# Forget terms of a forgetting-attention layer: added by VectorE from broadcast rows instead of by TensorE, with the heads' loads in GpSimd's queue

## The chip, the cores and the metric

The kernel runs on one core of one Trainium2 chip. The metric is the device time of one execution in microseconds (us). Engines are named as in the profile: PE is TensorE (PEld its weight loads), DVE is VectorE, ACT is ScalarE, POOL is GpSimd, SP is SyncE. A measurement is the median of several runs.

## The reference

One layer of a hybrid decoder over 512 tokens and 2048 channels, all in float32: a wide input projection feeds a gated short convolution and a forgetting attention with 8 heads of 128 channels; their gated sum is projected back, and a squared-ReLU MLP with 8192 hidden channels follows. The change touches the attention alone:

```
log_f = jax.nn.log_sigmoid(f_logit + b_f)             # (512, 8)
c = jnp.cumsum(log_f, axis=1)                         # per head
...
logits = jnp.einsum('bhqd,bhkd->bhqk', qb, kh) * scale
logits = logits + cb[..., :, None] - c[..., None, :]  # c of the query's row, minus c of the key
logits = jnp.where(causal, logits, -jnp.inf)
p = jax.nn.softmax(logits, axis=-1)
return jnp.einsum('bhqk,bhkd->bhqd', p, vh)
```

## The kernel before, in words

Nearly all the time goes to large matrix products. A product is worked in `Group`s: a group multiplies by a 2048 x 512 piece of weights in the seven-product (Strassen) manner. Its blocks are called A11, A12, A22 and S1 to S4, and each block's product has 48 matmuls of 256 columns (L164, L166 and L168 in `mm_rows` and `mm_cols`, accumulators a to d). A block of weights is loaded on SP's queue (L221), in places summed with another by DVE (L124), and then split into a high part `th` by ACT (L110) and a low part `tl` by DVE (L113, 2.3 us for 2048 columns). DVE adds products from PSUM to results (L127), ACT copies others (L252).

The attention stage lies between 255 and 480 us of the span. Before it, q and k of all heads were stored to DRAM as `kq_d` and v as `v_d`. It begins with the forget logits `fl`: ACT and DVE form their log-sigmoid `lf` (L784 to L787), PE sums it along the sequence by a product with a triangle `ut` (`pc`, L794), and DVE keeps the negative as `ncT` [8 heads, 512] (L796). Its transpose `cn` has the query's own term. `cparts` holds `ncT` in three bfloat16 parts, and `sel` for each head a matrix of ones that picks the head's rows out of it (L810 to L827), so that PE can add the key's term to the scores.

`attend(h)` computes one head. Three loads bring kT, qT and vv, 256 KB each (L837 to L840). For each of four tiles of 128 queries PE forms the scores in a PSUM bank (L846), adds the forget term `sel` x `cparts` (L847) and the causal mask (L848); tile 1 has 128 keys, tile 4 has 512. DVE takes the maximum (L850), ACT the exponential straight from PSUM with the row's sum (L856), DVE the reciprocal and the scaling (L858, L859), PE the transposes (L862, `tp`), DVE copies them to SBUF (`pt`, L864), and PE multiplies by vv into one bank `o` (L866). ACT copies `o` to `ov`, which POOL's queue stores to `a_d` (L869). The score tiles take turns in two banks (5 and 7). All SBUF tiles of `attend` come out of one ring of six buffers (tag "at", L777).

The loop at L948 goes over the conv branch's six groups. Ahead of each of the first four it issues the attention of two heads, so a round of the stage is two heads beside one group. A group stores its results through POOL's queue as `z_d` (L951). The order of instructions on each engine is set by the scheduler, by its own estimates, not by the order in which they are written; each engine and each DMA queue then works in order. The results of the stage are first wanted in later groups.

Of the kernel before, what the change touches and what calls it, by code (L numbers as in the profile page):

```python
# [8 lines left out]
F32 = mybir.dt.float32  # L9
F32R = mybir.dt.float32r  # L10
BF16 = mybir.dt.bfloat16
AF = mybir.ActivationFunctionType
ALU = mybir.AluOpType
AX = mybir.AxisListType

P = 128
S = 512
D = 2048
KT = D // P
NT = S // P  # L20
# [4 lines left out]
NH = AW // P  # L25
DFF = 4 * D
EPS = 1e-6
NEG = -1.0e30
# [17 lines left out]
def tile_hybrid_block(ctx: ExitStack, tc, x, g_mix, w_in, b_f, b_gate, conv_w, w_conv_out,  # L46
                      w_attn_out, w_mix_out, g_mlp, w_ff1, w_ff2, g_final, out):
    nc = tc.nc
    x, out = x[0], out[0]
# [4 lines left out]
    stat = ctx.enter_context(tc.tile_pool(name="stat", bufs=2))  # L54
# [3 lines left out]
    dram = ctx.enter_context(tc.tile_pool(name="dram", bufs=1, space=bass.MemoryType.DRAM))  # L58

    def phase(name):  # L60
        return tc.tile_pool(name=name, bufs=1, reuse_waits="tile")

    def bank(i, name):
        return psum.tile([P, S], F32, tag=f"p{i}", name=name)
# [7 lines left out]


    v_d = dram.tile([NT, P, AW], F32, name="v_d")
    kq_d = dram.tile([2, NH, P, S], F32, name="kq_d")
    z_d = dram.tile([3, CT, P, S], F32, name="z_d")
    g_d = dram.tile([2, KT, P, S], F32, name="g_d")
# [9 lines left out]
    warm = const.tile([P, 1], F32, name="warm")  # L87
# [8 lines left out]
    fl = const.tile([P, NT, NH], F32, name="fl")  # L96
# [605 lines left out]
    a, b = (gV0.acc(k)[0] for k in "ab")  # L702
# [71 lines left out]
    ph = ExitStack()  # L774
    pb = ph.enter_context(phase("pb"))

    def at(name, shape=None, dt=F32):  # L777
        return pb.tile(shape or [P, S], dt, tag="at", name=name, bufs=6)


    fa = const.tile([P, NT, NH], F32, name="fa")
# [1 line left out]
    nc.scalar.activation(out=fa, in_=fa, func=AF.Exp, scale=-1.0)  # L783
    nc.scalar.activation(out=fa, in_=fa, func=AF.Ln, bias=1.0)  # L784
    lf = const.tile([P, NT, NH], F32, name="lf")
    nc.vector.tensor_scalar(out=lf, in0=fl, scalar1=0.0, scalar2=None, op0=ALU.min)
    nc.vector.tensor_tensor(out=lf, in0=lf, in1=fa, op=ALU.subtract)  # L787
    ut = at("ut")
    nc.gpsimd.memset(ut, 1.0)
    nc.gpsimd.affine_select(out=ut[:, :P], in_=ut[:, :P], compare_op=ALU.is_ge, fill=0.0, base=0,  # L790
                            pattern=[[1, P]], channel_multiplier=-1)
    pc = bank(4, "pc")
    for t in range(NT):
        nc.tensor.matmul(pc[:NH, t * P:], lf[:, t, :], ut[:, :S - t * P], start=(t == 0), stop=(t == NT - 1))  # L794
    ncT = at("ncT", [NH, S])
    nc.vector.tensor_scalar(out=ncT, in0=pc[:NH, :], scalar1=-1.0, scalar2=None, op0=ALU.mult)  # L796
    pcn = bank(5, "pcn")
    for t in range(NT):
        nc.tensor.transpose(pcn[:, t * NH:(t + 1) * NH], ncT[:, t * P:(t + 1) * P], ident[:NH, :NH])
    cn = const.tile([P, NT, NH], F32, name="cn")  # L800
    nc.vector.tensor_scalar(out=cn.rearrange("p t h -> p (t h)"), in0=pcn[:, :NT * NH], scalar1=-1.0, scalar2=None,
                            op0=ALU.mult)
    identb = const.tile([P, P], BF16, name="identb")
# [3 lines left out]
    nc.gpsimd.affine_select(out=maskb, in_=maskb, compare_op=ALU.is_ge, fill=NEG, base=0,  # L807
                            pattern=[[-1, P]], channel_multiplier=1)

    cparts = pb.tile([96, S], BF16, name="cparts")  # L810
    nc.gpsimd.memset(cparts, 0.0)
    c1 = at("c1", [NH, S])
    nc.vector.tensor_copy(cparts[0:NH, :], ncT)
    nc.vector.tensor_tensor(out=c1, in0=ncT, in1=cparts[0:NH, :], op=ALU.subtract)
    nc.vector.tensor_copy(cparts[32:32 + NH, :], c1)
    c1b = at("c1b", [NH, S], BF16)
    nc.vector.tensor_copy(c1b, c1)
    c2 = at("c2", [NH, S])
    nc.vector.tensor_tensor(out=c2, in0=c1, in1=c1b, op=ALU.subtract)
    nc.vector.tensor_copy(cparts[64:64 + NH, :], c2)  # L820
    sel = pb.tile([96, NH, P], BF16, name="sel")
    nc.gpsimd.memset(sel, 0.0)

    nc.vector.memset(warm, 1.0)
    for b in range(3):
        nc.scalar.activation(out=sel[32 * b:32 * b + NH, :, :], in_=identb[0:NH, 0:NH].unsqueeze(2).to_broadcast([NH, NH, P]),
                             func=AF.Copy, scale=warm[0:NH, :])  # L827

    mt = [0]

    def m1(name):
# [1 line left out]
        return bank(4 + mt[0] % 4, name)  # L833

    def attend(h):
        kT, qT = at("kT"), at("qT")
        nc.sync.dma_start(out=kT, in_=kq_d[0, h])  # L837
        nc.sync.dma_start(out=qT, in_=kq_d[1, h])
        vv = at("vv", [P, NT, P])
        nc.sync.dma_start(out=vv, in_=v_d[:, :, h * P:(h + 1) * P].rearrange("t p c -> p t c"))  # L840
        o = bank(4, "o")
        for qi in range(NT):
            n = (qi + 1) * P
            qs = slice(qi * P, n)
            sc = bank(5 + 2 * (qi % 2), "sc")
            nc.tensor.matmul(sc[:, :n], qT[:, qs], kT[:, :n], start=True, stop=False)  # L846
            nc.tensor.matmul(sc[:, :n], sel[:, h, :], cparts[:, :n], start=False, stop=False)  # L847
            nc.tensor.matmul(sc[:, qs], identb, maskb, start=False, stop=True)  # L848
            nm = stat.tile([P, 1], F32, tag="nm", name="nm")
            nc.vector.tensor_reduce(out=nm, in_=sc[:, :n], axis=AX.X, op=ALU.max, negate=True)  # L850
            bias = stat.tile([P, 1], F32, tag="bias", name="bias")
            nc.vector.scalar_tensor_tensor(out=bias, in0=nm, scalar=cn[:, qi, h:h + 1], in1=cn[:, qi, h:h + 1],
                                           op0=ALU.subtract, op1=ALU.add)
            p = at("p")
            sm = stat.tile([P, 1], F32, tag="sm", name="sm")
            nc.scalar.activation(out=p[:, :n], in_=sc[:, :n], func=AF.Exp, bias=bias, accum_out=sm)  # L856
            rs = stat.tile([P, 1], F32, tag="rs", name="rs")
            nc.vector.reciprocal(out=rs, in_=sm)  # L858
            nc.vector.tensor_scalar(out=p[:, :n], in0=p[:, :n], scalar1=rs, scalar2=None, op0=ALU.mult)  # L859
            tp = bank(6, "tp")  # L860
            for ki in range(qi + 1):
                nc.tensor.transpose(tp[:, ki * P:(ki + 1) * P], p[:, ki * P:(ki + 1) * P], ident)  # L862
            pt = at("pt")
            nc.vector.tensor_copy(pt[:, :n], tp[:, :n])  # L864
            for ki in range(qi + 1):
                nc.tensor.matmul(o[:, qs], vv[:, ki, :], pt[:, ki * P:(ki + 1) * P], start=(ki == 0), stop=(ki == qi))  # L866
        ov = at("ov")
        nc.scalar.activation(out=ov, in_=o, func=AF.Copy)
        nc.gpsimd.dma_start(out=a_d[h], in_=ov)  # L869

# [76 lines left out]
    n = 0  # L947
    for g in (4, 2, 0, 5, 3, 1):  # L948
        def put_z(i, j, v, g=g, n=n):
            f = 4 * (g % 2) + 2 * j  # L950
            nc.gpsimd.dma_start(out=z_d[g // 2, f:f + 2, :, i * HS:(i + 1) * HS].rearrange("b p c -> p b c"), in_=v)  # L951
            signal(n, i, j, v)

        if n < NH // 2:
            for h in (2 * n, 2 * n + 1):
                attend(h)
        if n == NH // 2:
            ph.close()
            ph = ExitStack()
            pq = ph.enter_context(phase("pq"))  # L960
        ahead(n)
        whole(Group(w_in, g * S, g * S + HS, HS, Q1.moving, mm_cols, steady(n), put_z,
                    extra={} if n < NH // 2 else {"A11": "first", **apart(4, "S2", 0)}))
        behind(n)
        n += 1
# [235 lines left out]
    n = turns[0] + 1  # L1201
# [497 lines left out]
```

## Time and profile before

| | us |
|---|---|
| runs: median of 3 | 2445.77 |
| runs: lowest, highest | 2439.77, 2447.11 |
| the profiled execution's own time | 2440.54 |
| its span in the trace | 2438.7 |
| PE busy in the span | 2407.2 |
| DVE busy | 2043.1 |
| ACT busy | 1205.4 |
| POOL busy | 281.0 |

Rows of the trace read as follows: start in us, duration in us, engine, line, operation, output<-inputs, partitions x elements and type, count. In brackets stands the idle time before and what ended it. A group of instructions has its busy time and the mean in ns of one. The rows of transfers end with the KB of one and the median us from issue to landing. The windows cut the span into stretches and give for each the busy us of every engine, the granted clock of TensorE as a share (PEclk), the share of the DMA engines and GB/s. The chain of waits goes back from the last instruction, at each step to what released it.

### The profile page before, as it was taken

Reading aid. Unit: us, or ns where it says so; the run is one execution under the profiler, and the core shown is the slowest. Engines: PE = TensorE matmul, PEld = TensorE weight load, DVE = VectorE, ACT = ScalarE, POOL = GpSimd, SP = SyncE. Lnnn points to the kernel's source line nnn. Section 1 sums busy time; section 2 is a strip of 40 time slices with the busy share of each in tenths; the row PEclk is TensorE's granted clock in tenths of the full one; section 3 lists DMA queues with packets and bytes.
Section 4 is the critical chain, followed back from the end, with each engine's and each line's share of the span. In section 5 each row is a group of like instructions: output and inputs, shape, how many; then the busy total and the mean of one; then the engine's idle time right before and its main releaser. Section 6 shows DMA issues by size and latency. Waiting matters only on the chain.

```text
span 2438.7 us, 41547 instructions
## 1 busy us (share of the span) xinstructions
PE 2407.2 (99%) x17815; PEld 2263.2 (93%) x17815; DVE 2043.1 (84%) x1715; ACT 1205.4 (49%) x1233; POOL 281.0 (12%) x449
## 2 busy tenths in 40 slices
PE   9999999999999999999999999999999999999998
PEld 9999899999999999899999999999998888888886
DVE  7987777788887778888889888898887888889898
ACT  6444443345455445355656665666655333333334
POOL 1100000111121111113300000000011001100000
PEclk9999999999999999999999999999999999999999
DMA  8565544454656665657854665646587566655662
GB/s 267 176 189 152 155 127 139 139 164 163 212 171 216 210 205 166 218 163 249 318 197 174 219 213 200 233 170 222 210 300 282 166 234 235 231 198 178 245 225 103
DMA packets 283785, 489.89 MB, mean 201 GB/s; under 512 B 11668, under 2 KB 195056, under 8 KB 283216
## 3 DMA queue, kind: packets, MB, share of 16 engines
q1 hardware_dynamic: 232912, 279.01, 36.3%
q0 software_dynamic: 50080, 207.16, 22.8%
q8 instruction: 140, 2.29, 0.4%
q10 hardware_dynamic: 608, 1.06, 0.1%
q14 instruction: 45, 0.37, 0.0%
HBM read 377.60 MB, written 109.05 MB: 200 GB/s over the span
## 4 chain that ended last, share of the span: by engine, by line
PE 87%; DVE 5%; issue 3%; DMA 2%; ACT 1%; POOL 1%; SPq 0%; DVEq 0%; POOLq 0%; ACTq 0%
PE a L168 6%; PE a L164 6%; PE a L166 6%; PE d L168 5%; PE d L164 5%; PE d L166 5%; PE a L187 5%; PE a L185 5%; PE a L183 5%; PE c L164 4%; PE c L166 4%; PE c L168 4%; PE d L187 3%; PE d L185 3%; PE d L183 3%
## 5 line engine op out<-in xcount | busy, mean ns | idle before, releaser
L110 ACT ACTIVATE th<-x 128x2048 fp32r<-128x2048 f32 (+1 forms) x280 | 537.2, 1919 | 514.8 <-DVE x L124 173.9
L113 DVE TENSOR_TENSOR tl<-x,th 128x2048 fp32r<-128x2048 f32 (+2 forms) x282 | 639.5, 2274 | 161.9 <-ACT th L110 146.8
L124 DVE TENSOR_TENSOR x<-x,x 128x2048 f32<-128x2048 f32 (+1 forms) x160 | 366.2, 2288 | 23.7 <-DMA x<-in_w_in_dram 16.7
L110 ACT ACTIVATE th<-y 128x2048 fp32r<-128x2048 f32 (+1 forms) x109 | 185.7, 1704 | 274.3 <-PE a L185 138.6
L113 DVE TENSOR_TENSOR tl<-y,th 128x2048 fp32r<-128x2048 f32 (+1 forms) x109 | 219.1, 2015 | 29.8 <-ACT th L110 29.4
L183 PE MATMUL a<-th,us 128*128 128x512 f32 x512 | 199.3, 389 | 1.3 <-ACT th L110 1.3
L185 PE MATMUL a<-th,us 128*128 128x512 f32 x512 | 199.2, 389 | 0.0
L164 PE MATMUL c<-S,th 128*128 128x256 f32 x848 | 196.6, 277 | 0.7 <-ACT th L110 0.7
L166 PE MATMUL c<-S,th 128*128 128x256 f32 x848 | 196.2, 277 | 0.0
L164 PE MATMUL a<-S,th 128*128 128x256 f32 x784 | 182.2, 278 | 0.8 <-ACT th L110 0.8
L166 PE MATMUL a<-S,th 128*128 128x256 f32 x784 | 180.7, 276 | 0.0
L164 PEld LDWEIGHTS c<-S,th 128*128 128x128 f32 x848 | 159.3, 188 | 1.1 <-ACT th L110 0.8
L166 PEld LDWEIGHTS c<-S,th 128*128 128x128 f32 x848 | 159.3, 188 | 0.0
L164 PEld LDWEIGHTS a<-S,th 128*128 128x128 f32 x784 | 147.2, 188 | 1.0 <-ACT th L110 1.0
L166 PEld LDWEIGHTS a<-S,th 128*128 128x128 f32 x784 | 147.3, 188 | 0.0
L187 PE MATMUL a<-tl,us 128*128 128x512 f32 x512 | 136.9, 389 | 0.6 <-DVE tl L113 0.6
L166 PE MATMUL b<-A,th 128*128 128x256 f32 x544 | 126.6, 278 | 0.0
L164 PE MATMUL b<-A,th 128*128 128x256 f32 x544 | 126.5, 277 | 0.0
L164 PE MATMUL d<-S,th 128*128 128x256 f32 x544 | 126.4, 278 | 0.0
L164 PE MATMUL a<-A,th 128*128 128x256 f32 x544 | 126.2, 277 | 0.0
L166 PE MATMUL a<-A,th 128*128 128x256 f32 x544 | 126.1, 277 | 0.0
L166 PE MATMUL d<-S,th 128*128 128x256 f32 x544 | 125.8, 277 | 0.0
(405 smaller groups left out, 6063.3 us busy)
## 6 DMA issues: line engine op xcount, KB each, us to landing
x<-in_w_in_dram SPq DMA_DIRECT2D x86, 1024.0 KB, 5.8
y<-in_w_ff_dram SPq DMA_DIRECT2D x64, 1024.0 KB, 7.7
x<-in_w_ff_dram SPq DMA_DIRECT2D x60, 1024.0 KB, 8.5
us<-s_d POOLq DMA_DIRECT2D x48, 1024.0 KB, 9.2
s_d<-rh POOLq DMA_DIRECT2D x32, 896.0 KB, 5.7
s_d<-r POOLq DMA_DIRECT2D x32, 896.0 KB, 5.9
x<-in_w_mix_out_dram SPq DMA_DIRECT2D x17, 1024.0 KB, 7.2
g_d<-o POOLq DMA_DIRECT2D x32, 256.0 KB, 2.9
```

The source lines that it names most:

```text
L110: return tied(nc.scalar.activation(out=hi, in_=src, func=AF.Copy))
L113: return tied(nc.vector.tensor_tensor(out=lo, in0=src, in1=hi.bitcast(F32), op=ALU.subtract))
L124: return nc.vector.tensor_tensor(out=out, in0=a, in1=b, op=ALU.subtract)
L164: nc.tensor.matmul(o, hi[:, q, js], Sh, start=first and q == 0 and j == 0, stop=False, skip_group_check=True)
L166: nc.tensor.matmul(o, hi[:, q, js], Sl, start=False, stop=False, skip_group_check=True)
L168: nc.tensor.matmul(o, lo[:, q, js], Sh, start=False, stop=q == nq - 1, skip_group_check=True)
L183: tied(nc.tensor.matmul(o, Sh, hi[:, q, :], start=begin and q == 0, stop=False, skip_group_check=True))
L185: tied(nc.tensor.matmul(o, Sl, hi[:, q, :], start=False, stop=False, skip_group_check=True))
L187: tied(nc.tensor.matmul(o, Sh, lo[:, q, :], start=False, stop=q == nq - 1, skip_group_check=True))
```

## The change

The forget term of a key is no longer added by PE. `ncT` is stored to a DRAM tile `c_d`, and each head loads its row of it laid over all 128 partitions (`cb`). In place of the maximum, DVE runs a `tensor_tensor_reduce`: it computes the negative of (scores + cb), writes it to the SBUF tile `p`, and keeps the row's least in `m`; in the program it is two instructions, the second 128 x 1. The exponential then works within `p` with scale -1. L847, `cparts`, `sel` and their set-up (six DVE and three ACT operations and some memsets) are gone. `lf` is one operation instead of two. kT, qT, cb and vv have one buffer each, `p` and `pt` two each, in place of the ring of six; `ut` and `ncT` use `pt`'s, `ov` uses `p`'s. All loads of a head are in POOL's queue instead of SP's.

```diff
+    c_d = dram.tile([NH, S], F32, name="c_d")
...
-    def at(name, shape=None, dt=F32):
-        return pb.tile(shape or [P, S], dt, tag="at", name=name, bufs=6)
+    def at(tag, name=None, shape=None, bufs=1):
+        return pb.tile(shape or [P, S], F32, tag=tag, name=name or tag, bufs=bufs)
...
-    nc.vector.tensor_scalar(out=lf, in0=fl, scalar1=0.0, scalar2=None, op0=ALU.min)
-    nc.vector.tensor_tensor(out=lf, in0=lf, in1=fa, op=ALU.subtract)
-    ut = at("ut")
+    nc.vector.scalar_tensor_tensor(out=lf, in0=fl, scalar=0.0, in1=fa, op0=ALU.min, op1=ALU.subtract)
+    ut = at("pt", "ut", bufs=2)
...
-    ncT = at("ncT", [NH, S])
+    ncT = at("pt", "ncT", [NH, S], bufs=2)
     nc.vector.tensor_scalar(out=ncT, in0=pc[:NH, :], scalar1=-1.0, scalar2=None, op0=ALU.mult)
+    nc.gpsimd.dma_start(out=c_d, in_=ncT)
...
     def attend(h):
-        kT, qT = at("kT"), at("qT")
-        nc.sync.dma_start(out=kT, in_=kq_d[0, h])
-        nc.sync.dma_start(out=qT, in_=kq_d[1, h])
-        vv = at("vv", [P, NT, P])
-        nc.sync.dma_start(out=vv, in_=v_d[:, :, h * P:(h + 1) * P].rearrange("t p c -> p t c"))
+        kT, qT, cb, vv = at("kT"), at("qT"), at("cb"), at("vv", shape=[P, NT, P])
+        nc.gpsimd.dma_start(out=kT, in_=kq_d[0, h])
+        nc.gpsimd.dma_start(out=qT, in_=kq_d[1, h])
+        nc.gpsimd.dma_start(out=cb, in_=c_d[h:h + 1, :].to_broadcast([P, S]))
+        nc.gpsimd.dma_start(out=vv, in_=v_d[:, :, h * P:(h + 1) * P].rearrange("t p c -> p t c"))
...
-            nc.tensor.matmul(sc[:, :n], sel[:, h, :], cparts[:, :n], start=False, stop=False)
             nc.tensor.matmul(sc[:, qs], identb, maskb, start=False, stop=True)
-            nm = stat.tile([P, 1], F32, tag="nm", name="nm")
-            nc.vector.tensor_reduce(out=nm, in_=sc[:, :n], axis=AX.X, op=ALU.max, negate=True)
+            p = at("p", bufs=2)
+            m = stat.tile([P, 1], F32, tag="nm", name="m")
+            nc.vector.tensor_tensor_reduce(out=p[:, :n], in0=sc[:, :n], in1=cb[:, :n], scale=-1.0, scalar=-NEG, op0=ALU.add,
+                                           op1=ALU.min, accum_out=m)
...
-            p = at("p")
...
-            nc.scalar.activation(out=p[:, :n], in_=sc[:, :n], func=AF.Exp, bias=bias, accum_out=sm)
+            nc.scalar.activation(out=p[:, :n], in_=p[:, :n], func=AF.Exp, bias=bias, scale=-1.0, accum_out=sm)
...
-            pt = at("pt")
+            pt = at("pt", bufs=2)
...
-        ov = at("ov")
+        ov = at("p", "ov", bufs=2)
```

The scheduler also puts the instructions in another order. PE before, in the third round: the second head's first scores (sc_4127, sc_4146) stand among the products of the block S1 (accumulator c), 29 products behind the first head's last output, and each tile has the forget term's product (sel).

```order
L164 MATMUL c_4337<-S1_907,th_4338 128x256
L166 MATMUL c_4337<-S1_907,th_4338 128x256
L846 MATMUL sc_4127<-kT_4120,qT_4121 128x128 [waits DMAHW7_49,DMAHW6_49,Activation_49]
L847 LDWEIGHTS sel_2805
L847 MATMUL sc_4127<-cparts_2794,sel_2805 128x128
L848 LDWEIGHTS identb_2787
L848 MATMUL sc_4127<-maskb_2789,identb_2787 128x128
L846 MATMUL sc_4146<-kT_4120,qT_4121 128x256 [waits Activation_49]
```

PE in the changed program, in the same round: the second head's first scores (sc_4103, sc_4121) stand right behind the first head's second output (o_4006 from pt_4041), among the products of the block A11.

```order
L848 MATMUL o_4006<-pt_4022,vv_4001 128x128 [waits DMASW0_49,DVE_49]
L844 MATMUL tp_4038<-ident_90,p_4028 128x128 x2
L169 MATMUL a_4194<-A11_128,tl_4196 128x256 x6
L848 MATMUL o_4006<-pt_4041,vv_4001 128x128 [waits DVE_49]
L848 MATMUL o_4006<-pt_4041,vv_4001 128x128
L828 MATMUL sc_4103<-kT_4094,qT_4095 128x128 [waits DMASW6_49,DMASW5_49,PE_49]
L829 LDWEIGHTS identb_2788
L829 MATMUL sc_4103<-maskb_2790,identb_2788 128x128
L828 MATMUL sc_4121<-kT_4094,qT_4095 128x256 [waits DVE_49,PE_49]
```

So they moved ahead, past the first head's third and fourth transposes and outputs and most of two blocks of products.

The queues of the loads, SP before: the loads of two heads (kT_4022, kT_4120 and their fellows) stand between the loads of weights (x11 and others).

```order
L837 DMA kT_4022<-kq_d_70 128x512 [waits DMASW4_49,DMASW0_49,PE_49]
L838 DMA qT_4023<-kq_d_70 128x512 [waits DMAHW3_49,DMASW3_49,DMAHW5_49,DMASW2_49,PE_49]
L840 DMA vv_4026<-v_d_69 128x4x128 [waits DMASW3_49,DMAHW4_49,DVE_49,PE_49]
L221 DMA x11_4334<-in_w_in_dram 128x8x256 [waits DVE_49]
L837 DMA kT_4120<-kq_d_70 128x512 [waits DMAHW6_49,DVE_49,PE_49]
L838 DMA qT_4121<-kq_d_70 128x512 [waits DMAHW3_49,DMAHW7_49,DVE_49,PE_49]
L840 DMA vv_4124<-v_d_69 128x4x128 [waits DMAHW0_49,DMAHW2_49,DVE_49,PE_49]
```

POOL in the changed program: the second head's four loads (kT_4094 to vv_4097) follow one another, behind the stores of a group (z_d) and ahead of the first head's store (a_d) and of the next round's loads (kT_4587).

```order
L933 DMA z_d_72<-o_3884 128x2x256 [waits DMASW4_49,DVE_49]
L819 DMA kT_4094<-kq_d_71 128x512 [waits DMASW5_49,PE_49]
L820 DMA qT_4095<-kq_d_71 128x512 [waits DMASW6_49]
L821 DMA cb_4096<-c_d_70 128x512 [waits DMASW7_49,DVE_49]
L822 DMA vv_4097<-v_d_69 128x4x128 [waits DMASW0_49,PE_49]
L851 DMA a_d_78<-ov_4091 128x512 [waits DMASW1_49,Activation_49]
L819 DMA kT_4587<-kq_d_71 128x512 [waits DMASW5_49,DMASW2_49,PE_49]
L820 DMA qT_4588<-kq_d_71 128x512 [waits DMASW6_49,DMASW3_49]
```

So they left SP's queue, which keeps the weights alone, and each of them now waits, by its one buffer, for the engine that last read it for the head before.

More of the change, by code (lines that the diff above doesn't have):

```diff
@@ L808, in tile_hybrid_block @@
                             pattern=[[-1, P]], channel_multiplier=1)
[L810 to L827, printed above, removed]
     mt = [0]
@@ L846, in attend @@
             nc.tensor.matmul(sc[:, :n], qT[:, qs], kT[:, :n], start=True, stop=False)
-            nc.tensor.matmul(sc[:, :n], sel[:, h, :], cparts[:, :n], start=False, stop=False)
             nc.tensor.matmul(sc[:, qs], identb, maskb, start=False, stop=True)
-            nm = stat.tile([P, 1], F32, tag="nm", name="nm")
-            nc.vector.tensor_reduce(out=nm, in_=sc[:, :n], axis=AX.X, op=ALU.max, negate=True)
+            p = at("p", bufs=2)
+            m = stat.tile([P, 1], F32, tag="nm", name="m")
+            nc.vector.tensor_tensor_reduce(out=p[:, :n], in0=sc[:, :n], in1=cb[:, :n], scale=-1.0, scalar=-NEG, op0=ALU.add,
+                                           op1=ALU.min, accum_out=m)
             bias = stat.tile([P, 1], F32, tag="bias", name="bias")
-            nc.vector.scalar_tensor_tensor(out=bias, in0=nm, scalar=cn[:, qi, h:h + 1], in1=cn[:, qi, h:h + 1],
+            nc.vector.scalar_tensor_tensor(out=bias, in0=m, scalar=cn[:, qi, h:h + 1], in1=cn[:, qi, h:h + 1],
                                            op0=ALU.subtract, op1=ALU.add)
-            p = at("p")
             sm = stat.tile([P, 1], F32, tag="sm", name="sm")
-            nc.scalar.activation(out=p[:, :n], in_=sc[:, :n], func=AF.Exp, bias=bias, accum_out=sm)
+            nc.scalar.activation(out=p[:, :n], in_=p[:, :n], func=AF.Exp, bias=bias, scale=-1.0, accum_out=sm)
             rs = stat.tile([P, 1], F32, tag="rs", name="rs")
```

## Prediction

> **What bounds the kernel now.** I read the page's engine shares first, then the waits of TensorE (PE) in the attention stage, which is the only stage that the change touches, and then the stage cut into its four rounds. A round is two heads of attention woven into one group of products for the conv branch; I call the two heads of a round A and B.
>
> ```profile
> PE 2407.2 (99%) x17815; PEld 2263.2 (93%) x17815; DVE 2043.1 (84%) x1715; ACT 1205.4 (49%) x1233; POOL 281.0 (12%) x449
> ```
>
> PE is busy 99% of the 2438.7 us span, so only what PE issues and what it waits for can move the end. In the stage (255 to 480 us) its largest waits are these; the columns are the sum, the count and the longest:
>
> ```profile
> engine line waited for: us in total, times, longest us
> PE sc L846 <- DMA qT<-kq_d: 1.8, 1, 1.8
> PE pc L794 <- DVE lf L787: 1.3, 1, 1.3
> ```
>
> ```profile
> core 0: us, PE busy (x) PEld busy (x) DVE busy (x) ACT busy (x) POOL busy (x), PEclk, DMA share, GB/s
> 264.00:317.00 53.00, 51.23 (x407) 47.11 (x406) 39.79 (x63) 22.32 (x30) 3.31 (x5) 1.00 0.47 145
> 317.00:371.00 54.00, 53.87 (x431) 50.32 (x430) 38.30 (x57) 21.27 (x30) 4.00 (x6) 1.00 0.44 137
> ...
> 425.00:479.00 54.00, 53.72 (x426) 50.00 (x426) 39.03 (x56) 20.72 (x30) 7.41 (x14) 1.00 0.46 141
> ```
>
> So 3.1 us of waits in 225 us are to be had, in and just ahead of the first round, in which PE idles 1.8 us; rounds two and four (and three like two) have PE idle for 0.1 to 0.3 us. VectorE (DVE) has some 15 us free in each round, ScalarE (ACT) over 30, and the granted clock is 1.00 throughout. What the change saves elsewhere than on PE is worth nothing by itself.
>
> **PE's own work: the forget term's products (L847) go.** Matmuls overlap, so I cost one by the time from its start to the start of the next. The third round's first head has all four:
>
> ```profile
> 371.04 0.38 PE L846 MATMUL sc<-kT,qT 128*128 128x128 f32 x2
> 371.26 0.22 PE L847 MATMUL sc<-cparts,sel 96*128 96x128 bf16 x1
> 371.32 0.22 PE L848 MATMUL sc<-maskb,identb 128*128 128x128 bf16 x1
> ...
> 371.86 0.27 PE L847 MATMUL sc<-cparts,sel 96*128 96x256 bf16 x1
> 371.98 0.22 PE L848 MATMUL sc<-maskb,identb 128*128 128x128 bf16 x1
> ...
> 375.67 0.33 PE L847 MATMUL sc<-cparts,sel 96*128 96x384 bf16 x1
> 375.84 0.22 PE L848 MATMUL sc<-maskb,identb 128*128 128x128 bf16 x1
> ...
> 380.63 0.38 PE L847 MATMUL sc<-cparts,sel 96*128 96x512 bf16 x1
> 380.85 0.22 PE L848 MATMUL sc<-maskb,identb 128*128 128x128 bf16 x1
> ```
>
> The slots are 0.06, 0.12, 0.17 and 0.22 us, 0.57 per head, **1.13 per round**, 4.5 for eight heads. Busy time (0.22 + 0.27 + 0.33 + 0.38 = 1.2 per head) would promise twice as much.
>
> **VectorE's new operation.** The maximum (L850) becomes one operation that adds the broadcast row, writes the sum to SBUF and keeps the least, with a second, one-column instruction behind it. The trace has no such operation. The nearest rows are the reduction it replaces, a two-input sum from PSUM, and ACT's read of its accumulator:
>
> ```profile
> L850 DVE TENSOR_REDUCE nm<-sc 128x1 f32<-128x512 f32 x8 | 5.4, 677 | 0.0
> L127 DVE TENSOR_TENSOR o<-b,o 128x512 f32<-128x512 f32 x4 | 2.8, 692 | 7.4 <-PE b L168 7.4
> L856 ACT ACTIVATION_READ_ACCUMULATOR p<-sc,bias 128x1 f32 x32 | 6.2, 194 | 0.0
> ```
>
> At 512 columns 692 + 194 = 0.89 us against 0.68 is the upper bound by these rows (+0.2 a tile), 692 alone the lower (+0.02), and two passes over the tile (twice 0.68) the bound beyond. I take +0.1, nearest to the two-input row: 0.8 per round, on an engine with 15 us free, beside products. It counts at nothing, and the cover's loss is a rival below. The exp then reads SBUF instead of PSUM on an ACT that is half idle: nothing.
>
> **What this does to the order.** In exchange a score bank is free once DVE has read it, not once ACT has. In the trace the third tile's forget product stands 4.6 us and the fourth's 9.6 us behind the head's first score (371.04). Here the DVE part of that chain:
>
> ```profile
> 373.03 0.69 DVE L127 TENSOR_TENSOR o<-d,o 128x512 f32<-128x512 f32 x1
> 373.63 0.61 DVE L850 TENSOR_REDUCE nm<-sc 128x1 f32<-128x128 f32 x2
> 374.42 2.29 DVE L113 TENSOR_TENSOR tl<-x,th 128x2048 fp32r<-128x2048 f32 x1
> ...
> 377.68 0.27 PE L862 MATMUL tp<-ident,p 128*128 128x128 f32 x1
> ...
> 392.50 0.38 PE L846 MATMUL sc<-kT,qT 128*128 128x128 f32 x2
> ```
>
> Call the first score's start T. DVE reaches the first two tiles at T+2.6 and has read them by about T+3.6; then the 2.3 us split, the softmax and the first transpose at T+6.6, as before. With banks free at T+2.9 and T+3.6, the third and fourth scores run by T+4.6. The changed program puts head B's first score right behind A's second output (the rows above, in the section on the change): 40 products of the group at 0.118 us (4.7), A's scores (2.5) and its first transposes and outputs (1.0) stand ahead of it, 8.2 in all, 0.8 more for the wait on the first transposes' operands: **T+8.95**, where it stood at T+21.5 (392.50).
>
> **The loads.** kT, qT and vv now have one buffer each and go through GpSimd's queue, so B's kT is issued only after A's fourth scores, T+4.7, and qT an issue later (0.54, the second row below), T+5.25. How long they take is the disputed number; the last column is us from issue to landing:
>
> ```profile
> L951 POOL DMA_DIRECT2D z_d<-o x24: 710/724/740, 274.2 to 561.9; - x24
> L890 POOL DMA_DIRECT2D cb<-z_d x8: 539/539/557, 469.0 to 707.4; - x8
> ```
>
> ```profile
> kT<-kq_d SPq DMA_DIRECT2D x8, 256.0 KB, 4.4
> qT<-kq_d SPq DMA_DIRECT2D x8, 256.0 KB, 3.3
> xr<-in_x_dram POOLq DMA_DIRECT2D x16, 256.0 KB, 4.0
> merged<-held_d POOLq DMA_DIRECT2D x8, 256.0 KB, 8.3
> a_d<-ov POOLq DMA_DIRECT2D x8, 256.0 KB, 2.5
> ```
>
> Bounds for 256 KB: 3.3 (qT) below, 8.3 (merged, the slowest in GpSimd's queue) above. I take 4.4, kT's own and near xr's 4.0 in the queue that is now used. qT lands at T+9.65 and PE waits **0.7** (nothing at 3.3; 4.6 at 8.3). vv is held until A's fourth output, T+15.8, lands at T+20.2, and B's first output is due at T+19.25: **0.95** (nothing at 3.3). The row cb is held by A's fourth reduction, T+9.15, and is wanted at T+14.6, so it has 5.4 us and is covered unless it takes longer. By the Trainium skill, "DMA: Bandwidth & Descriptors", section "Anatomy of one DMA — SWDGE (gpsimd) path", a transfer takes about 2.0 us plus its bytes over 436 GB/s, an estimate of 2.6 us here, at which neither load would be late and each round 1.65 us shorter; this case's trace has 4.0 for the same size in that queue, and the sum goes by the trace.
>
> Behind a waiting kT on GpSimd's queue stand qT, cb, vv, the head's store and the next z_d store; the waits for the stores' landing (a_d 2.5 us) fall in a time in which nobody needs their data. SP keeps only the weights; PE waits for none, so nothing is won there.
>
> **The first round.** Its own waits go and one comes:
>
> ```profile
> 257.97 0.23 ACT L784 ACTIVATE fa<-fa 128x32 f32<-128x32 f32 x1
> 260.04 2.29 DVE L113 TENSOR_TENSOR tl<-x,th 128x2048 fp32r<-128x2048 f32 x1 [1.38 <-ACT th L110]
> 262.25 0.19 DVE L787 TENSOR_TENSOR lf<-lf,fa 128x32 f32<-128x32 f32 x1
> ```
>
> lf's second operation stood behind a 2.3 us split; as one operation it stands ahead, ready near 258.7, and PE's 1.3 us goes. The 1.8 us for qT are replaced by the 0.7 above. New is a path through DRAM. ncT stands behind two DVE operations of 2.3 us that follow lf, and takes some 0.7 itself (as L127 above): 264.0; then a store of 2.5 and a load of 4.4, so cb is there near 271, where PE wants the third score near 270 (its bank needs the first reduction): **+1.4**, between 0 and 3. Round one: −1.3 − 1.8 − 1.13 + 0.7 + 0.95 + 1.4 = −1.2. DVE's six setup operations and ACT's `sel` also go; PE waited for neither.
>
> **Sum.** Rounds two to four: −1.13 + 0.7 + 0.95 = +0.5 each, +1.6; with the first **+0.4 us**. The profiled execution took 2440.54, so 2440.9; the median of the runs (2445.77) lies 5.2 above it, which gives 2446. One more bound: the group's products run at two speeds in this stage,
>
> ```profile
> 471.96 1.88 PE c L168 x16
> 477.62 1.88 PE d L168 x16
> ...
> 488.70 1.81 PE b L168 x16
> 494.14 1.81 PE c L168 x16
> ```
>
> 48 products in 5.66 us or, after the stage, in 5.44. A changed rhythm can move up to 1344 of them to the other speed, −6 us. I forecast no change of speed, with ±6 about 2446.
>
> **Rivals.** (A, slower) **B's loads land late.** Place: kT and qT, one buffer each, behind one another in a shared queue. At 6 us, midway between the rows' ends, qT lands at T+11.25 (2.3 late) and vv, shifted with PE, 2.55 late: 4.9 per round instead of 1.65, 3.2 × 4 = +13: 2459. It exceeds 7 us from a landing of about 5.3 us on. For it: merged's 8.3 and four loads issued together. Against: xr's 4.0, kT's 4.4. (B, faster) **Loads at 3.3 or less, nobody waits**, −1.65 × 4, and about half of the products go to the faster speed, −3: 2436. For it: qT's row; against: kT's. (C, slower) **The custom reduction takes two passes**: 1.9 us more per head on DVE; the first two (0.7) stand ahead of the first transpose, so 0.7 to 1.9 × 8 = 5.6 to 15: about 2456. Nothing in the trace decides it. (D) **The change moves the loads but they are held while DVE works.** A kT issue at T+4.7 falls into the split of 2.29 us that starts at T+3.4 to T+3.9; held to its end (T+6.1) it costs 1.4 × 4 = +6: 2452. Against: 24 stores issued beside the same splits took 710 to 740 ns, none long. The Trainium skill's "SBUF — State Buffer", section "SBUF: two separate sides", says that a GpSimd DMA cannot get its descriptors written while a VectorE copy holds the shared port, 620 ns becoming about 3100; the issues of this trace show no such thing.
>
> **How the numbers follow.** Forecast 0.50, A 0.23, B 0.14, C 0.08, D 0.05. A measurement of this kernel can tell about 0.3%, 7.3 us, from no change. Slower by more: 0.20 of A, 0.06 of C, 0.02 of D, 0.02 of the forecast's edge, 0.30. Faster by more: 0.13 of B and 0.02 of the edge, 0.15. Within: 0.55. The range is 2433 to 2461: it holds B and the forecast, and of A and C all but landings beyond 6.2 us and the upper half of C; the forecast's own range is 2440 to 2452.
>
> **What would show it.** Right: PE's wait for lf gone; waits of the scores on kT/qT and of o on vv of under 1.5 us in each round; a broadcast cb landing in the first round just late; rounds within 1 us of the 54 that the windows above have. Wrong: loads of over 5.3 us (A), below 3.6 (B), a reduction at 512 columns of over 1.2 us (C), issues of over 2 us on POOL (D), or a different speed of the products in the stages behind, which I take as untouched.

## The result and the profile after

The changed kernel takes 2434.5 us (median of 7 runs, 2432.9 to 2435.7) against 2441.1 for the kernel before (median of its 7 runs, the three shown above among them): ratio **0.9967, 95% interval 0.9958 to 0.9976**, 6.6 us faster by the medians. Run again beside later experiments it had 0.9956 (0.9943 to 0.9968). The profiled execution took 2433.25 us with a span of 2431.4, so 7.3 us less than the span of before. One execution of a later kernel (e13) took 4040 us at a mean granted clock of 0.556, where all others have 0.995 to 0.999, and is left out.

Where the time went is seen from two marks on PE. The first product of the stage's group starts at 257.56 before and at 258.26 after; the 192-column product with which the group behind the stage begins is this row, before and after:

```profile
479.34 0.25 PE L157 MATMUL a<-A,th 128*128 128x192 f32 x1
```

```profile
472.81 0.25 PE L158 MATMUL a<-A,th 128*128 128x192 f32 x1
```

The stage went from 221.8 us to 214.5, **−7.2 us** (of which 0.5 is one score tile that now stands ahead of the first mark); what lies behind it went from 1959.4 to 1958.6. So the stage holds nearly all of it. The rounds after, cut at the first score of each; the columns are those of the prediction's windows:

```profile
core 0: us, PE busy (x) PEld busy (x) DVE busy (x) ACT busy (x) POOL busy (x), PEclk, DMA share, GB/s
264.00:313.80 49.80, 49.00 (x396) 45.82 (x395) 34.85 (x62) 22.25 (x30) 9.15 (x15) 1.00 0.54 158
313.80:366.30 52.50, 52.07 (x422) 48.74 (x421) 39.89 (x65) 21.46 (x30) 8.77 (x14) 1.00 0.50 151
366.30:419.75 53.45, 52.84 (x422) 49.42 (x421) 40.16 (x66) 21.72 (x30) 8.78 (x14) 1.00 0.48 149
```

Rounds two and three take 52.5 and 53.4 us where they took 53.6 and 53.8; the fourth (419.75 to 472.81) 53.1 where it took 54.5; the rest, some 4 us, came out of the first. PE's waits in the stage are now all small:

```profile
engine line waited for: us in total, times, longest us
PE sc L828 <- DVE m L832: 0.8, 3, 0.3
PE o L848 <- DMA vv<-v_d: 0.4, 2, 0.2
PE tp L844 <- DVE rs L840: 0.2, 1, 0.2
PE sc L828 <- DMA qT<-kq_d: 0.2, 1, 0.2
```

Gone are the waits for lf (1.3) and for the first round's qT (1.8), and little came: 1.6 us in all, of which loads are 0.6, where the prediction had 8.0 for loads (0.7 and 0.95 in each of four rounds, and 1.4 for cb). The loads' own rows say why; the last column is the median from issue to landing:

```profile
vv<-v_d POOLq DMA_DIRECT2D x8, 256.0 KB, 3.7
qT<-kq_d POOLq DMA_DIRECT2D x8, 256.0 KB, 3.1
kT<-kq_d POOLq DMA_DIRECT2D x8, 256.0 KB, 3.0
cb<-c_d POOLq DMA_DIRECT2D x8, 256.0 KB, 3.5
```

The new operation of VectorE and its read of the accumulator, in the stage:

```profile
L832 DVE CUSTOM_DVE_ANT_0 p<-sc,cb 128x512 f32<-128x512 f32 x8 | 5.4, 680 | 0.0
L832 DVE DVE_READ_ACCUMULATOR2_ANT m<- 128x1 f32 x32 | 2.6, 82 | 0.0
```

680 ns against 677 for the maximum it replaces, and 82 ns more.

One new wait stands on VectorE and not on PE. `ov` now takes one of `p`'s two buffers, so VectorE's operation on the second head's third tile waits for the first head's store to land, 1.6 to 1.7 us in each of rounds two to four (third round here):

```profile
386.82 0.56 DVE L832 CUSTOM_DVE_ANT_0 p<-sc,cb 128x384 f32<-128x384 f32 x1 [1.67 <-DMA a_d<-ov]
```

PE's share of it is within the 0.8 us that it waits for `m`.

### The profile page after: what moved, and what is told of

It reads as the page before. It is cut to its first block, busy times and chain, and to the rows that moved or that the text cites. A ratio compares the mean times of both kernels' runs of the same rounds, so it can differ in the third digit from the quotient of the medians.

```text
span 2431.4 us, 41446 instructions
## 1 busy us (share of the span) xinstructions
PE 2404.7 (99%) x17783; PEld 2262.7 (93%) x17783; DVE 2041.5 (84%) x1739; ACT 1201.7 (49%) x1230; POOL 299.4 (12%) x480
## 4 chain that ended last, share of the span: by engine, by line
PE 86%; DVE 5%; issue 3%; DMA 3%; ACT 1%; POOL 1%; SPq 0%; DVEq 0%; POOLq 0%; ACTq 0%
PE a L165 6%; PE a L169 6%; PE a L167 6%; PE a L188 5%; PE d L165 5%; PE a L186 5%; PE a L184 5%; PE d L167 5%; PE d L169 5%; PE c L165 4%; PE c L167 4%; PE c L169 4%; PE d L188 3%; PE d L186 3%; PE d L184 3%
```

## The experiments

Each kernel stands against the kernel before on its own chip. The ratio is that of the medians, with its 95% interval. "Stage" is the time between the two marks above in the kernel's profiled execution, "waits" the sum of PE's waits in it. Two executions of the changed kernel agree in this column to 0.1 us and two of the version with SP's queue to 1.4, so differences below 1.5 us are not read. Behind the stage these executions take between 1955.9 and 1962.9 us with no pattern that I can name, so the stage is steadier than the total. Nearly every edit also lets the scheduler reorder PE: of the 1693 PE instructions that the stage has without the forget (or zero) products, some 230 stand elsewhere in e1, 80 in e4 and 30 in e7, against before, and 180 in e2, 170 in e6, 270 in e8, 220 in e9, 60 in e12, 50 in e13 and 30 in e3 and e11, against the changed kernel; none do in e10.

| kernel | ratio | median us | stage | waits |
|---|---|---|---|---|
| before | 1 | 2441.1 | 221.8 | 3.4 |
| changed | 0.9967 (0.9958 to 0.9976) | 2434.5 | 214.5 | 1.6 |
| changed, again (e5) | 0.9956 (0.9943 to 0.9968) | 2430.7 | 214.5 | 2.4 |
| e1: before without L847 | 0.9980 (0.9971 to 0.9989) | 2436.2 | 217.4 | 4.0 |
| e2: changed, zero product | 1.0015 (1.0006 to 1.0024) | 2444.7 | 222.0 | 4.8 |
| e3: changed, loads on SP | 0.9963 (0.9951 to 0.9974) | 2432.1 | 212.8 | 1.9 |
| e11: the same again | 0.9961 (0.9947 to 0.9975) | 2434.4 | 211.4 | 0.9 |
| e4: before, loads on GpSimd | 1.0046 (1.0033 to 1.0060) | 2452.9 | 231.2 | 11.9 |
| e6: changed, kT twice | 0.9979 (0.9969 to 0.9988) | 2437.6 | 217.4 | 6.2 |
| e7: before, lf in one | 0.9996 (0.9987 to 1.0004) | 2441.1 | 221.0 | 3.6 |
| e8: changed, reduction twice | 0.9984 (0.9976 to 0.9993) | 2439.1 | 219.6 | 8.7 |
| e9: changed, plain maximum | 0.9979 (0.9970 to 0.9988) | 2436.1 | 217.7 | 5.8 |
| e10: changed, copy of 1 MB | 0.9968 (0.9958 to 0.9979) | 2434.4 | 213.8 | 2.3 |
| e12: changed, copy of 2 MB | 0.9969 (0.9957 to 0.9981) | 2433.9 | 214.2 | 2.7 |
| e13: changed, qT late | 0.9962 (0.9949 to 0.9975) | 2432.1 | 214.4 | 1.5 |

**Theories.** Theory 1: the gain is PE's slots of the forget products and the first round's waits, and the loads cost nothing. Theory 2: the gain comes from the loads leaving SP's queue. Theory 3: the spacing of the group's products changed.

**e1, the forget product alone.**

```diff
-            nc.tensor.matmul(sc[:, :n], sel[:, h, :], cparts[:, :n], start=False, stop=False)
```

> The kernel before without L847; the key's forget term is left out of the scores, everything else (cparts, sel, loads on SP's queue, the maximum by DVE, the exponential from PSUM) stays. Theory 1 (the gain is PE's slots of the forget products, 0.565 us per head, and the first round's waits): 4.5 us faster than before, ratio 0.9982, near 2436.6, rounds two to four about 1.1 us shorter, the first round's waits for lf and qT still there. Theory 2 (the gain comes from the loads leaving SP's queue): under 1 us faster, since a score that ends sooner only waits for its loads. Theory 3 (the products' spacing, 113 against 118 ns, changed with the order): no fixed sign, up to 6 us either way, seen in the spacing of 16 products and not in the waits.

The stage lost 4.4 us, the median 5.1. The wait for lf is there as before. One for qT is as long as before, but it stands in the second round (at 349.38) and no longer in the first (300.59):

```profile
PE sc L846 <- DMA qT<-kq_d: 1.9, 1, 1.9
PE pc L794 <- DVE lf L787: 1.3, 1, 1.3
```

So PE's slots are worth 4.4 us without anything else of the change, as the prediction's 4.5 had it, and Theory 2 is not needed for them. The order on PE moved too, but its waits stayed about the same, 4.0 us against 3.4.

**e2, the product back in the changed kernel.**

```diff
+    zp = pb.tile([96, 32], BF16, name="zp")
+    nc.gpsimd.memset(zp, 0.0)
...
+            nc.tensor.matmul(sc[:, :n], identb[0:96, :], zp.unsqueeze(1).to_broadcast([96, n // 32, 32]), start=False,
+                             stop=False)
             nc.tensor.matmul(sc[:, qs], identb, maskb, start=False, stop=True)
```

> The changed kernel with a product of the forget product's size (96 rows, bfloat16, 128 to 512 columns) of zeros put back into each score group, so PE has its old work and all else is new. Theory 1: 4.5 us slower than the changed kernel, near 2439, rounds longer by 1.1 us each, waits as in the changed kernel. Theory 2: as fast as the changed kernel within 1 us. Theory 3: undetermined, to be read from the spacing of the products.

A miss: the stage became 7.5 us longer, not 4.5, and the whole kernel 10.2 by the medians. The products themselves take 4.5 (each from its start to the next start, summed over the trace). The rest are waits, 4.8 us instead of 1.6:

```profile
PE sc L831 <- issue: 1.6, 1, 1.6
PE sc L831 <- DVE m L837: 1.3, 4, 0.7
PE o L853 <- DMA vv<-v_d: 1.3, 3, 0.5
PE sc L831 <- DMA qT<-kq_d: 0.6, 3, 0.2
```

The 1.6 us that the list calls "issue" are one late load as well. The second round's qT was issued at 321.96 and landed 4.6 us later, at 326.57, just ahead of this row:

```profile
326.66 0.46 PE L831 MATMUL sc<-kT,qT 128*128 128x128 f32 x2 [1.62 <-issue]
```

So loads make up 3.5 of the 4.8 us, half of it in this one place. There the load itself was slow: kT stands 5.6 us behind the first head's first score (321.40 behind 315.82), where the changed kernel has 5.4. 4.5 + 3.2 = 7.7 against 7.5 measured: what came late was paid about in full.

**e3 and e11, the queue in the changed kernel.**

```diff
-        nc.gpsimd.dma_start(out=kT, in_=kq_d[0, h])
+        nc.sync.dma_start(out=kT, in_=kq_d[0, h])
```

and the same for qT, cb and vv.

> The changed kernel with the heads' four loads (kT, qT, cb, vv) back in SP's queue, single buffers kept. Theory 1 with my landing times of the prediction (4.4 us by SP's queue, 3.0 to 3.7 by GpSimd's in the changed trace): the loads land about 1 us later, so 0.7 to 1.4 us of waits per round and 3 to 6 us slower than the changed kernel, near 2438 to 2440. If the queue decides nothing and 3.0 is what an unhurried load takes on either: within 1 us of the changed kernel. Theory 2: 5 us or more slower, with the wait of the first round for qT (1.8 us) back.

> The changed kernel with the heads' four loads in SP's queue, once more: the fastest version so far. If GpSimd's queue costs 1 to 2 us of this change: 2430 to 2433. If the earlier difference was that of chips and rounds: as the changed kernel, 2431 to 2435.

Theory 2 falls: with the loads back on SP's queue the stage is 1.8 and 3.1 us shorter, not longer. Where these come from is not shown: PE's waits are 1.9 and 0.9 us against 1.6; VectorE's waits for the store of `ov` are 4.2 and 2.2 us against 5.4. The loads of kT and qT land a little sooner on SP's queue (attention stage of e3):

```profile
kT<-kq_d SPq DMA_DIRECT2D x7, 256.0 KB, 2.7
qT<-kq_d SPq DMA_DIRECT2D x7, 256.0 KB, 3.0
```

My own expectation from the 4.4 us of the prediction falls with it: the same queue as in the kernel before now has 2.7. In total time the two versions with SP's queue are not told from the changed kernel (0.9961 and 0.9963 against 0.9956 and 0.9967).

**e4, the queue in the kernel before.** The three loads moved to GpSimd's queue, with no other edit.

> The kernel before with kT, qT and vv loaded by GpSimd's queue out of the same ring of six buffers; all else as before. Theory 1: only the first round's wait for qT goes, 1 to 2 us faster than before, near 2439.5. Theory 2: 5 us or more faster, near 2435. No gain at all would say that the wait for qT is not made by SP's queue.

Against both theories: 11.6 us slower. PE waits 9.4 us for qT, and the queue shows what stood ahead of it (second round):

```profile
339.65 0.57 POOL L837 DMA_DIRECT2D kT<-kq_d  x1
343.56 0.56 POOL L869 DMA_DIRECT2D a_d<-ov  x1 [3.34 <-ACT ov L868]
344.11 0.54 POOL L838 DMA_DIRECT2D qT<-kq_d  x1
```

```profile
350.53 0.46 PE L846 MATMUL sc<-kT,qT 128*128 128x128 f32 x2 [3.69 <-DMA qT<-kq_d]
```

qT stands behind the store of the head before, which waits 3.3 us for ScalarE's `ov`; it then takes 6.3 us to land. I put this order down to the ring of six buffers, which no run changes alone; in the changed kernel kT and qT follow one another (371.68 and 372.24 in the third round).

**e6, kT loaded twice**, the second load behind the landing of the first:

> The changed kernel with kT of each head loaded twice into its one buffer, the second load behind the first, so that kT and the qT behind it land some 3.5 us later; the data are the same. It prices rival A of the prediction, that the second head's loads are late. Theory 1 (the loads just make it, landing within 0.2 us of the second head's first score, so that any more delay is paid in full): 3 to 3.5 us per round, 12 to 14 in all, near 2447, with waits of PE for qT of about 3 us in each round. Rival (a delay of PE here is absorbed, because what PE waits for later in the round, VectorE's reductions and vv, has caught up): 4 to 8 us in all, near 2441.

2.9 us in the stage: it fits neither number. (By the medians it is 3.1 us slower than the first measurement of the changed kernel and 6.8 slower than the one on the same chip, e5, so the total does not decide.) PE waits for kT in each round, but by 0.6 to 1.0 us:

```profile
PE sc L829 <- DMA kT<-kq_d: 3.1, 4, 1.0
```

The scheduler put the second head's scores 11.4 us behind the first head's (316.32 to 327.76) where the changed kernel has 9.1 (313.79 to 322.86), with products of the group in between. So this kernel does not price a late load in a fixed order.

**e7, lf in one operation** in the kernel before:

```diff
-    nc.vector.tensor_scalar(out=lf, in0=fl, scalar1=0.0, scalar2=None, op0=ALU.min)
-    nc.vector.tensor_tensor(out=lf, in0=lf, in1=fa, op=ALU.subtract)
+    nc.vector.scalar_tensor_tensor(out=lf, in0=fl, scalar=0.0, in1=fa, op0=ALU.min, op1=ALU.subtract)
```

> The kernel before with lf in one operation, as the change has it, and nothing else. Theory 1: the 1.3 us that PE waits for lf go, 1.0 to 1.5 us faster than before, near 2440. Rival: ncT and the heads' first scores stand behind the same two 2.3 us operations of VectorE as before, and PE waits there instead: no change.

The wait for lf is gone, but PE waits 1.0 us a little later for ncT; the stage is 0.8 us shorter, within its scatter, and the total cannot tell it from nothing (0.9987 to 1.0004).

```profile
PE pcn L798 <- DVE ncT L795: 1.0, 1, 1.0
```

**e8, the combined operation twice in a row.**

> The changed kernel with the combined operation of VectorE run twice in a row with the same result, so 1.9 us (and four times 0.08) more of VectorE for each head in the chain between scores and exponential; it prices rival C of the prediction. Theory 1 (VectorE has 14 us free per round and the added work lies beside products): under 2 us slower than the changed kernel in all. The prediction's price (0.7 to 1.9 us for each head): 5.6 to 15 us slower, 2438 to 2449, with waits of PE for m, rs or pt in each round.

Theory 1's "beside products" falls: the stage is 5.1 us longer, 0.63 per head for 1.93 + 4 x 0.08 = 2.3 us of added VectorE work. PE's waits are what the prediction's rival C named:

```profile
PE sc L828 <- DVE m L834: 5.3, 6, 2.0
PE o L850 <- DMA vv<-v_d: 1.8, 2, 1.1
```

So VectorE is not covered in this stage in spite of some 13 us of idle time per round. The 0.63 us are the price of the added work and of the order that the scheduler made of it together: in the second round the second head's first score stands 13.5 us behind the first head's (329.59 behind 316.09), where the changed kernel has 9.1. The change itself costs little there because its operation is only 0.09 us longer than the one that it replaces.

**e9, the plain maximum and the exponential from PSUM** in the changed kernel, without cb and without any product for the key's term, which is left out:

```diff
-            nc.vector.tensor_tensor_reduce(out=p[:, :n], in0=sc[:, :n], in1=cb[:, :n], scale=-1.0, scalar=-NEG, op0=ALU.add,
-                                           op1=ALU.min, accum_out=m)
+            nc.vector.tensor_reduce(out=m, in_=sc[:, :n], axis=AX.X, op=ALU.max, negate=True)
...
-            nc.scalar.activation(out=p[:, :n], in_=p[:, :n], func=AF.Exp, bias=bias, scale=-1.0, accum_out=sm)
+            nc.scalar.activation(out=p[:, :n], in_=sc[:, :n], func=AF.Exp, bias=bias, accum_out=sm)
```

> The changed kernel with the plain maximum from PSUM and the exponential from PSUM again, and without cb: the key's forget term is left out, no product for it on PE either. Loads, buffers and lf are those of the change. Theory 1 (the combined operation costs what the maximum did, and cb is covered): within 1.5 us of the changed kernel, near 2434.5. Rival (releasing the score banks by VectorE instead of ScalarE, and the order that the scheduler makes of it, is itself a part of the gain): 3 us or more slower than the changed kernel, near 2438 or above, with waits of PE for p (ScalarE) or for loads that come later.

The rival holds: 3.1 us more in the stage, although this kernel does less. A score bank is again held until ScalarE has read it (1.6 us of waits), and PE waits 3.7 us for vv:

```profile
PE o L846 <- DMA vv<-v_d: 3.7, 4, 1.0
PE sc L827 <- ACT p L836: 1.6, 2, 1.4
```

In the second round vv is issued at 334.19, 17.3 us behind the first head's first score (316.93), where the changed kernel has 16.0 (329.79 behind 313.79); it is asked for at 337.0 and there at 337.9. I read this so: the earlier release of the banks, which the prediction only followed for its effect on the order, is what lets a single buffer for vv do. As the order on PE changed with it, the 3.1 us are the price of both together.

**e10 and e12, a copy from DRAM to DRAM beside the load of vv,** of 1 MB and of 2 MB, released by the first head's third tile:

```diff
+            if h % 2 == 0 and qi == 2:
+                nc.gpsimd.dma_start(out=busy_d[:, 0:1], in_=bias)
+                nc.gpsimd.dma_start(out=busy_d, in_=w_in[0:P, 0:4 * S])
```

> The changed kernel with one copy of 1 MB from DRAM to DRAM in GpSimd's queue in each round, released by the first head's third tile, so that it moves while vv of the second head is loaded; PE's order of instructions is the changed kernel's, row for row. Theory 1 (loads land in 3 to 4 us when the DMA engines are half idle and in 6 to 8 us when they are full, and with a late vv PE waits for the difference): vv of the second head lands 6 to 8 us from its issue, PE waits 2.5 to 4 us for it in each round, 8 to 14 us slower than the changed kernel, 2441 to 2448. Rival (what decides a load's time is its queue, not the traffic): vv lands within 4.5 us, under 3 us slower in all.

> As e10_busy_dma, but with a copy of 2 MB in each round, since the copy of 1 MB had landed (5.2 to 6.8 us after its issue) before vv of the second head was issued, and so told nothing of a load amid traffic. PE's order of instructions is the changed kernel's but for some 40 rows. Theory 1 (traffic sets a load's time): vv of the second head, issued about 5 us behind the copy, lands 5 to 8 us from its issue in each round instead of 3.7, PE waits 1.5 to 4 us for it, and the kernel is 5 to 14 us slower than the changed kernel, near 2440 to 2448. Rival (the queue sets it): vv within 4.5 us, under 3 us slower.

e10 told nothing of it: the copy landed between 0.1 us ahead of vv's issue and 1.0 us behind it, and vv took 3.5 to 3.7 us. In e12 vv was issued 5 to 7 us behind a copy that takes 8.5 to 9.6, and landed after 4.6, 3.8, 4.4 and 3.9 us; PE waited 1.6 us in all for vv, and the time is the changed kernel's. My 5 to 8 us were too high. The copy did not bring the traffic either that I wanted: the DMA share in the four microseconds from vv's issue on was 0.96 in the first round, and 0.58, 0.51 and 0.48 in the others.

**e13, eight elements of qT written once more** behind its landing, for the second head of each round:

> The changed kernel with eight elements of the second head's qT written once more, behind the landing of the load itself, so that qT is there some 2 to 2.5 us later; in rounds two to four PE's order differs only in that the second head's first score stands two products and three transposes further back (about 0.5 us). Theory 1 (a late load of the second head is paid in full, as the prediction's sum had it, and only the landing time was mis-sized): PE waits 1.5 to 2 us for qT in each round, 5 to 8 us slower than the changed kernel, near 2440. Rival (the price itself was wrong, because other waits of the round take the delay up): waits for qT are there, but other waits shrink by as much, under 3 us slower, near 2436.

It priced nothing. The eight elements belong to the first of the head's four tiles of queries, so only that tile's score had to wait for them, and the scheduler put it behind the second tile's (second round):

```profile
323.93 0.63 PE L830 MATMUL sc<-kT,qT 128*128 128x256 f32 x2
326.01 0.38 PE L830 MATMUL sc<-kT,qT 128*128 128x128 f32 x2
```

The second tile runs 8.9 us behind the first head's first score (315.00), where the changed kernel has the first tile at 9.1; here the first tile runs at 11.0, when its elements have landed (325.61). PE waits for neither.

## Why the prediction was wrong

The time lies in the range, near its low end, but the sign was not the one forecast: +0.4 us from before stood against −6.6. Of the 11.5 us between 2446 and 2434.5, 4.7 are the base (a median of 2445.77 over three runs, 2441.1 over seven); the others are the sum's. By its steps:

- **The forget products, 4.5 us: right.** e1 has 4.4 in the stage.
- **The first round's waits for lf and qT, 3.1 us: right** as to what goes. Of lf alone e7 keeps at most 0.8 of 1.3, since ncT is late next; with the change that wait is not there (the four rows above).
- **VectorE's operation at nothing: right in size, wrong in its reason.** 680 + 82 ns against 677 is +0.09 us, where I took +0.1. The cover that I named isn't one: e8 pays 0.63 us per head for 2.3, and with the change PE waits 0.8 us for `m`.
- **The stores: right for PE only.** The prediction had their landing fall in a time in which nobody needs their data; VectorE waits 5.4 us for it, as shown above.
- **The order: right.** The second head's first score was put at T+8.95 and is at T+8.9 to 9.2 in rounds two to four; kT's issue at T+4.7 and is at T+5.4 (319.20 behind 313.79); vv's at T+15.8 and is at T+16.0 to 16.1 in rounds two and three:

```profile
366.32 0.38 PE L828 MATMUL sc<-kT,qT 128*128 128x128 f32 x2
...
370.30 1.08 PE L828 MATMUL sc<-kT,qT 128*128 128x512 f32 x2
...
375.50 0.46 PE L828 MATMUL sc<-kT,qT 128*128 128x128 f32 x2
...
386.30 0.46 PE L848 MATMUL o<-pt,vv 128*128 128x128 f32 x2 [0.22 <-DMA vv<-v_d]
```

- **The step that failed: "I take 4.4, kT's own and near xr's 4.0 in the queue that is now used."** The loads that PE is about to need, the second heads', take 3.0 to 3.7. qT lands at T+5.9 + 3.1 = T+9.0 and vv at T+16.1 + 3.7 = T+19.8, each with at most 0.2 us of waiting, where the sum had 0.7 and 0.95 per round; cb lands at 270.1 (266.54 + 3.6), not 271, and PE does not wait for it. 8.0 us of waits were forecast for loads and 0.6 came. With the 1.0 us that PE waits for VectorE, 1.6 stand against 8.0; these 6.4 us are the miss, and 0.7 of faster spacing (below) make up about the rest of the 7.0.

The 4.4 was no duration that any load of before had. The median of eight lay in the gap between two groups, and a view of single loads shows both. Two loads of kT of the kernel before, each with its landing:

```profile
L837 SPq DMA_DIRECT2D kT<-kq_d x1: 521/521/521, 354.8 to 354.8; - x1
DMA to landing us min/median/max: 6.6/6.6/6.6
...
L837 SPq DMA_DIRECT2D kT<-kq_d x1: 332/332/332, 385.3 to 385.3; - x1
DMA to landing us min/median/max: 2.7/2.7/2.7
```

The four microseconds from each issue on, with the DMA share in the last column but one:

```profile
354.78:358.78 4.00, 3.99 (x34) 3.77 (x33) 1.20 (x3) 1.75 (x1) 0.00 (x0) 1.00 0.80 233
...
385.30:389.30 4.00, 4.00 (x35) 3.92 (x34) 1.81 (x4) 1.92 (x1) 0.00 (x0) 1.00 0.58 148
```

And what stood ahead of the slow one in SP's queue, a 1 MB load of weights, half a microsecond earlier:

```profile
354.31 0.37 SPq L221 DMA_DIRECT2D x<-in_w_in_dram  x1
354.78 0.52 SPq L837 DMA_DIRECT2D kT<-kq_d  x1
```

In the kernel before the eight loads of kT took 2.5, 2.7, 2.7 and 2.7 us at a DMA share of 0.55 to 0.58, and 6.2, 6.6, 6.9 and 7.4 at 0.80 to 0.83, each of these four right behind a 1 MB load. In the changed kernel the second heads' kT is issued five microseconds into a round, at a share of 0.43 in rounds two to four, and takes 2.9 to 3.1. That SP's queue by itself is not the cause is shown: e3 has 2.7 there. Nor must a load stand behind another in its own queue to be slow: in the changed kernel vv of a first head, issued at 349.76 in GpSimd's queue with no other transfer of that queue on its way, took 6.0 us at a share of 1.01, and kT at 142.92 took 5.4 at 0.94. So traffic is the likeliest cause, but it is not shown by an experiment, and the share alone does not set the time: e12 has a kT (288.91) of 3.6 us at 0.97 and e2 the qT of 4.6 us at 0.36.

So the first half of rival B came about (loads of kT and qT at 3.3 or less, hardly a wait; 2436 forecast), but not its second half: the mean spacing of the group's products, where one directly follows another, went from 115.9 to 115.3 ns, 0.7 us over some 1200 of them, which also leaves Theory 3 no more than that. Rival A needed loads like the slow four; rival D did not occur: kT's issue at 371.68 falls into VectorE's split from 369.96 on and takes 0.57 us.

```profile
371.68 0.57 POOL L819 DMA_DIRECT2D kT<-kq_d  x1 [1.42 <-PE sc L829]
```

```profile
369.96 2.28 DVE L114 TENSOR_TENSOR tl<-x,th 128x2048 fp32r<-128x2048 f32 x1
```

What the prediction took from the Trainium skill's "SBUF — State Buffer", section "SBUF: two separate sides", is said there of a VectorE copy. For a VectorE operation with two SBUF inputs, as this split is, the same section of the Trainium skill has GpSimd blocked only where it reads SBUF, and of a load's issue it names the writing of descriptors. So it gave rival D no support here, and the trace agrees: the issue was not held. The Trainium skill's "DMA: Bandwidth & Descriptors", section "Anatomy of one DMA — SWDGE (gpsimd) path", gives an estimate of 2.6 us for 256 KB; the trace has 2.9 to 3.1 for kT and qT in the quiet parts of the rounds, nearer to it than to what I took.

What stays open: what a late load of the second head costs in the changed kernel's own order. Where a load came late unforeseen (e2, e9) most or all of the wait was paid; in e6 the scores stood further back and little was paid. Only e10 keeps the order, and there nothing came more than 0.5 us late.

## What to carry to other kernels

Before a median duration goes into a sum, look at the single instances: with two groups, the one to take is that of the moment at which the transfer will be issued, judged by the DMA share there and by what stands ahead in its queue (here the two went together in the kernel before). An operation that reads a PSUM bank out for good releases it at that point; on a chain through several engines that, with the order that it allows, can be worth nearly as much as the work that is saved (here 3 us against 4.4). What a queue costs a load depends on what waits ahead of it: the same move to GpSimd's queue cost 11.6 us in the kernel where a waiting store came to stand ahead, and 2 to 3 us of the stage in the other.

## What was not expected of the hardware

Adding two operands and keeping the row's least costs VectorE what the plain maximum does: 281, 417, 550 and 680 ns at 128 to 512 columns against 284, 417, 547 and 677, with 82 ns for reading the accumulator. And idle time did not measure cover: VectorE had some 13 us free in each round, yet a quarter of what e8 added came out on the end.
